# Layer 2 of a two-layer trunk: compression operand layout, branch gates in the key block, second keys among the memory tiles, output projection prepared in steps

## The chip, the cores and the metric

The kernel runs on one core of one Trainium2 chip. The metric is device time in microseconds (us). The kernel before takes 1500.77 us, the median of three runs (1500.14 to 1501.25). The engines are named as in the profile: PE is TensorE's matmul, PEld its weight load, DVE is VectorE, ACT is ScalarE, POOL is GpSimd, and SP issues nearly all DMAs.

## The reference

The input is x of 1024 rows by 1024 columns in float32, and a memory of 256 rows. Both layers norm their input, project it with one wide matrix, run three token mixers, multiply each by its own SiLU gate, and project the concatenation of 1280 columns back to 1024, with a residual. Layer 1 has sliding-window attention, a linear recurrence (RG-LRU) and cross-attention into the memory. The change is in layer 2, whose mixers are HGRN2 (a chunked gated recurrence), native sparse attention (NSA) with 8 query heads in two key groups, and memory cross-attention. What NSA needs of the rest:

```
for t, pe, w1, w2 in keys, values:          # compression: 63 windows of 32 rows, stride 16
    flat = (t windows + pe).reshape(63, 32*64)
    c = silu(flat @ w1) @ w2
g = sigmoid(gate_logits)                    # 24 columns of the input projection
o = g0 * o_compressed + g1 * o_selected + g2 * o_window
```

## The kernel before

Each projection is done three times over: weights and activations are split into a high part and a rest (`split`, L240 on ACT, L246 on DVE or POOL), and `mm3` (L388 to L390) multiplies high by high, high by rest and rest by high. A `block` of weights is loaded in chunks of 512 words per partition: `chunk` issues one DMA for each run of columns (L352) and splits what has landed. With a width of n columns a chunk holds 512/n of the eight contraction slices. `proj_n` multiplies one tile of 128 rows (eight tiles in all) with a block of 256 columns; its result occupies one of three `pj` buffers until it is read out. `proj_t` gives 128 columns transposed for half of the rows (512).

The program writes the work down as generators that `weave` interleaves: a main generator, and sides of which a share falls due as main advances by one yield. A scheduler then fixes the order in which the instructions stand on each engine; each engine runs its own list in order. SP is one list too: a DMA that waits there holds those behind it.

Layer 2 begins while the last matmuls of layer 1's output projection run. `start` makes the first NSA keys and values (`nsa_kv(w, 0)`) and gates. Per tile `nsa_kv` projects, norms (L409, L411), rotates (L421 to L430), scales (L1177), copies the values out (L234, L236), transposes (`pairs`, L249) and stacks the keys (L449, L441). `nsa_gates` computes the 24 branch gates beside it: a separate block of 24 columns, two transposed projections with 24 stationary columns and 512 moving ones, a tanh over 24 by 512, and eight small transposes back. `compress` runs woven into this. For keys and for values it projects, copies the result out as `tT` with the 512 positions of each half-pair in order, moves it by DMA into `U`, and then runs 16 matmuls (L1258) whose moving operand takes every eighth word of `U`, 63 of each group. (In float32 the trace shows two records for each of these 32 matmuls.)

Then `main` runs: NSA with the first keys (65 yields), 4 yields of gates, 20 of memory attention (`pipe(tilesM)`), 9 of the second keys (`nsa_kv(w, 1)`), 4 of gates, 65 of NSA with the second keys. Beside it runs HGRN2 (`self.side`, with quarters due at yields 46, 68, 100 and 138), and the first half of the output projection (`out_proj`), 16 units due between yields 138 and 164. Its first step loads and splits all ten slices of the mixed rows (L1466, L1469, into `mhi` and `mlo`) and the first of four weight blocks. The second half of the output projection stands at the end by itself.

Of the kernel before, what the change touches and what calls it, by code (L numbers as in the profile page):

```python
# [5 lines left out]
F32 = mybir.dt.float32  # L6
# [8 lines left out]
P = 128  # L15
S = 1024
NT = S // P
# [8 lines left out]
LV1 = 4  # L26
T1 = 46
T2 = 68
T3 = 100
T4 = 138  # L30
SIDE = (0, T1, T2, T3, T4)
B_WHO = 6
NR1 = 3
OS = 26
B_PT = 6
B_GT = 1
B_HW = 6
# [11 lines left out]
E0 = 38  # L49
E1 = 46  # L50
E2 = 54
OG = 138
CY = 2
CK = 2
KV2 = 2
# [59 lines left out]
def drain(g):  # L115
    for _ in g:
        pass
# [25 lines left out]
class Trunk:  # L143
# [198 lines left out]
    def chunk(self, k, n, srcs, tag="whl"):  # L342

        nc = self.nc
        view = lambda t: t.rearrange("p (k n) -> p k n", k=k)
        self.nraw += 1
        if self.starting and self.nraw % 3:
            raw = view(self.hw("raw", [H]))
        else:
            raw = view(self.ring.tile([P, H], F32, tag="raw", name=self.uid("raw"), bufs=B_RAW))  # L350
# [3 lines left out]
        t = self.ring.tile([P, 2, H], F32R, tag=tag, name=self.uid("whl"), bufs=B_WHO if tag == 'who' else B_WHL)  # L354
        hi, lo = view(t[:, 0, :]), view(t[:, 1, :])
        self.split(hi[:, :, :n1], lo[:, :, :n1], raw[:, :, :n1])
        return hi, lo

    def block(self, w, pieces, rows=D, n=256, tag="whl"):

        k = H // n
        out = []
        for c in range(rows // (k * P)):
            at, srcs = 0, []
            for col, width in pieces:
                srcs.append((at, width, w[c * k * P:(c + 1) * k * P, col:col + width].rearrange("(k p) n -> p k n", p=P)))
                at += width
            out.append(self.chunk(k, n, srcs, tag))
        return out, k
# [538 lines left out]
    def layer1(self):  # L908
        nc, I, o = self.nc, self.I, OD
        w = I["od_w_in"][0]  # L910
        mix = {i: [None, None] for i in (2, 3, 4)}
        xs = {}

        def norms(half):
            for s in range(4 * half, 4 * half + 4, 2):
                for t in range(s, min(s + 4, 4 * half + 4)):
                    if t not in xs:
                        xs[t] = self.b4([D], name="h")
                        nc.sync.dma_start(xs[t], self.h1[t * P:(t + 1) * P, :])
# [12 lines left out]

        def start():
            yield from self.nsa_kv(w, 0)
            yield from self.gates(w, o["gd"], mix[2])

        first, later, gates = start(), norms(1), self.nsa_gates(w)
        for g in (later, first, first, gates, later, first, first, later, later, gates):
# [12 lines left out]
        drain(self.side)  # L951
        drain(self.out_proj(1, I["od_w_out"][0], 1, self.h1, self.out))

# [188 lines left out]
        nc.sync.dma_start(self.dkn[:, 1, :], I["d_kn_win"][0].partition_broadcast(P))  # L1142
        self.dkv = {}

    def nsa_gates(self, w):
        nc = self.nc
        self.bg = self.lc.tile([P, NT, 24], F32, name="bg")
        blk = self.block(w, [(OD["gate"], 24)], n=64)
        for half in range(2):
            ps = self.pj()  # L1150
            for k in range(KD):
                self.mm3(ps[0:24], self.wk(blk, k, 24), self.xhl(k, half, slice(0, H)), k == 0, k == KD - 1)
            th = self.gt("th", [H])
            nc.scalar.activation(th[0:24], ps[0:24], AF.Tanh, scale=0.5)
            pt = self.tr()
            for i in range(4):
                self.transpose(pt[:, i, 0:24], th[0:24, i * P:(i + 1) * P], 24)
            nc.vector.tensor_scalar(out=self.bg[:, 4 * half:4 * half + 4, :], in0=pt[:, :, 0:24], scalar1=0.5, scalar2=0.5,
                                    op0=ALU.mult, op1=ALU.add)
            yield  # L1160

    def nsa_kv(self, w, g):
        nc, o = self.nc, OD
        kS = [self.b4([S], F32R, name="kS") for _ in range(2)]
        vD = self.b4([NT, 2, HD], name="vD")
        self.dkv[g] = (kS, vD)
        blk = self.n_block(w, *[(o[n] + g * HD, HD) for n in ("ksd", "kwd", "vsd", "vwd")])
        zs, ks = {}, {}
        for s in range(NT + 2):
            if s < NT:  # L1170
                zs[s] = self.proj_n(blk, s)
            if 0 <= s - 1 < NT:
                z = zs.pop(s - 1)
                r = self.heads_norm(z[:, :P], 2, 1.0 / HD, EPS)
                k = self.rope(z[:, :P], 2, self.dkn, s - 1)
                k3 = k[:, :P].rearrange("p (h d) -> p h d", h=2)
                nc.vector.tensor_tensor(out=k3, in0=k3, in1=r[:, :, None].to_broadcast([P, 2, HD]), op=ALU.mult)  # L1177
                self.evac(vD[:, s - 1].rearrange("p b d -> p (b d)"), z[:, P:])
# [29 lines left out]
    def compress(self, w):  # L1208
# [9 lines left out]
        for kind in range(2):  # L1218
            blk = self.t_block(w, o["kcd" if kind == 0 else "vcd"])

            tT = self.tmp.tile([P, 2, H], F32, tag="qk", name=self.uid("tT"), bufs=1)
# [3 lines left out]
            U = self.tmp.tile([P, 2, H], F32, tag="qT", name=self.uid("U"), bufs=2)  # L1225
            for g in range(2):
                for u in range(2):
                    nc.sync.dma_start(U[u * HD:(u + 1) * HD, g, :], tT[g * HD:(g + 1) * HD, u, :])
            nm = "kv"[kind]
            w1 = [self.pt_tile("w1", [4 * 256]).rearrange("p (c n) -> p c n", c=8) for _ in range(2)]  # L1230
            for i in range(2):
                nc.gpsimd.tensor_copy(w1[i][0:1, 0, 0:1], tT[0:1, 0, 0:1])
# [217 lines left out]
        return dict(project=project, turn=turn, choose=choose, coarse=coarse, units=units)  # L1450


    def out_proj(self, l, w, half, resid, dst):

        nc = self.nc
        view = lambda x, q, i: x[half * H + i * P:half * H + (i + 2) * P, q * 256:(q + 1) * 256].rearrange("(i p) n -> p i n", p=P)
        hl, parts = [], (0, 1, 2, 4, 3) if l else range(5)
        for i in range(5):
            hi, lo = (self.b4([2, H], F32R, name=x) for x in ("mhi", "mlo"))
            for c in range(2):  # L1460
# [8 lines left out]
                nc.scalar.copy(hi[:, c, :], m)  # L1469
                nc.vector.tensor_tensor(out=lo[:, c, :], in0=m, in1=hi[:, c, :].bitcast(F32), op=ALU.subtract)  # L1470
            hl.append((hi, lo))
        for q in range(4):
            with self.tc.issue_after(self.loads) if l == 1 and half == 0 else nullcontext():
                blk = self.block(w, [(q * 256, 256)], rows=1280, tag='who' if l == 1 and half == 0 else 'whl')
# [86 lines left out]
```

## Time and profile before

| | us |
|---|---|
| median of three runs | 1500.77 |
| the profiled execution, its own time | 1501.38 |
| span of that execution in the trace | 1499.5 |
| PE busy in the span | 1424.4 (95%) |
| PEld, DVE, POOL, ACT busy | 1233.1, 870.0, 701.1, 657.1 |

Of the chain of work that ended last, the profile gives 82% of the span to PE, 7% to DVE, 4% to ACT and 3% to POOL. Read the table with care: a record of a matmul lasts from its start to its end while the next is already running, so what a matmul costs is the distance from one start to the next, which the timeline gives. The share of busy time is an average; the rows below are from the stages that the change touches.

### The profile page before, as it was taken

The page shows a single profiled execution, that of the slowest core. Times are in us where ns is not written, and L with a number is a line of the kernel's source. Part 1 is how long each engine was busy: PE and PEld are TensorE (multiplying, and loading weights), DVE is VectorE, ACT ScalarE, POOL GpSimd, SP SyncE. Part 2 cuts the span into 40 slices and gives each one's busy share as a digit, 9 for nine tenths or more (in the row PEclk, how much of TensorE's full clock was granted, in tenths as well). Part 3 has the DMA queues.
Part 4 walks back from the last instruction along what each step waited for, and adds up shares of the span by engine and source line. Part 5 has one row for each costly group of instructions (what it writes and reads, how often), then busy time and mean ns, then how long its engine had stood idle before and what let it go on. Part 6 is the DMA issues. An engine that isn't in the chain of part 4 may idle for free.

```text
span 1499.5 us, 27634 instructions
## 1 busy us (share of the span) xinstructions
PE 1424.4 (95%) x10107; PEld 1233.1 (82%) x10107; DVE 870.0 (58%) x2495; ACT 657.1 (44%) x1627; POOL 701.1 (47%) x1124
## 2 busy tenths in 40 slices
PE   7999999998699999999999999999989988899998
PEld 6888878787589988898777877798888866789898
DVE  6667886866763436326565565535664467655621
ACT  7545653645453433114444444423422245655630
POOL 6345675565653243114644444425742456444521
PEclk9999999999799999999999999999999989999999
DMA  8420131022445563310000100031020000423323
GB/s 291 123 65 1 57 85 43 30 64 71 136 132 179 184 168 85 86 41 18 12 22 22 50 8 22 16 91 45 22 78 1 8 1 8 141 66 127 105 82 109
DMA packets 120250, 108.55 MB, mean 72 GB/s; under 512 B 18825, under 2 KB 108466, under 8 KB 120114
## 3 DMA queue, kind: packets, MB, share of 16 engines
q1 hardware_dynamic: 119538, 104.68, 23.4%
q0 software_dynamic: 576, 2.10, 0.5%
q8 instruction: 80, 1.31, 0.4%
q14 instruction: 56, 0.46, 0.1%
HBM read 87.35 MB, written 18.35 MB: 70 GB/s over the span
## 4 chain that ended last, share of the span: by engine, by line
PE 82%; DVE 7%; ACT 4%; POOL 3%; issue 2%; DMA 1%; SPq 0%; ACTq 0%; POOLq 0%; DVEq 0%
PE pj L388 18%; PE pj L389 18%; PE pj L390 17%; PE tr L249 8%; PE ov L1432 5%; PE sc L468 3%; PE sc L469 2%; PE sc L1057 2%; DVE Pt L472 1%; PE sc L1258 1%; PE ov L658 1%; POOL Pt L797 1%; PE ov L805 1%; PE sc L390 1%; PE sc L388 1%
## 5 line engine op out<-in xcount | busy, mean ns | idle before, releaser
L388 PE MATMUL pj<-xn,whl 128*128 128x512 f32 (+1 forms) x536 | 213.4, 399 | 3.6 <-DVE fixed L421 1.4
L389 PE MATMUL pj<-xn,whl 128*128 128x512 f32 (+1 forms) x536 | 213.0, 398 | 0.0
L390 PE MATMUL pj<-xn,whl 128*128 128x512 f32 (+1 forms) x536 | 212.7, 397 | 0.0
L246 POOL TENSOR_TENSOR whl<-raw,whl 128x512 fp32r<-128x512 f32 x98 | 129.9, 1327 | 163.4 <-ACT whl L240 157.3
L388 PE MATMUL pj<-whl,xn 128*128 128x256 f32 x680 | 196.3, 289 | 0.0
L390 PE MATMUL pj<-whl,xn 128*128 128x256 f32 x680 | 196.0, 289 | 0.0
L389 PE MATMUL pj<-whl,xn 128*128 128x256 f32 x680 | 195.9, 288 | 0.0
L388 PE MATMUL pj<-whl,mhi 128*128 128x256 f32 x640 | 185.0, 292 | 11.1 <-ACT mhi L1469 5.3
L240 ACT CAST whl<-raw 128x512 fp32r<-128x512 f32 (+1 forms) x209 | 126.3, 619 | 148.0 <-PE pj L390 62.9
L389 PE MATMUL pj<-whl,mhi 128*128 128x256 f32 x640 | 184.9, 290 | 0.6 <-POOL whl L246 0.6
L390 PE MATMUL pj<-whl,mlo 128*128 128x256 f32 x640 | 182.1, 289 | 0.1
L1412 POOL TENSOR_SCALAR Pt<-Pt,fixed,lc 128x640 f32<-128x640 f32 (+7 forms) x128 | 105.2, 830 | 82.2 <-DVE fixed L1409 67.0
L388 PEld LDWEIGHTS pj<-whl,mhi 128*128 128x128 f32 x640 | 124.7, 196 | 13.4 <-ACT mhi L1469 5.8
L249 PE MATMUL tr<-fixed,Pt 128*128 128x128 f32 x776 | 127.4, 282 | 8.0 <-DVE fixed L472 2.7
L388 PEld LDWEIGHTS pj<-whl,xn 128*128 128x128 f32 x680 | 130.2, 192 | 4.6 <-issue 2.9
L389 PEld LDWEIGHTS pj<-whl,xn 128*128 128x128 f32 x680 | 130.2, 191 | 3.7 <-issue 2.1
L390 PEld LDWEIGHTS pj<-whl,xn 128*128 128x128 f32 x680 | 130.1, 191 | 1.4 <-issue 1.3
L389 PEld LDWEIGHTS pj<-whl,mhi 128*128 128x128 f32 x640 | 125.0, 195 | 3.0 <-issue 2.1
L1408 ACT ACTIVATE Pt<-Pt,fixed 128x640 f32<-128x640 f32 (+7 forms) x128 | 99.0, 775 | 60.4 <-DVE fixed L1405 34.5
L390 PEld LDWEIGHTS pj<-whl,mlo 128*128 128x128 f32 x640 | 123.8, 195 | 1.2 <-issue 0.9
L246 DVE TENSOR_TENSOR whl<-raw,whl 128x512 fp32r<-128x512 f32 x111 | 89.9, 814 | 58.5 <-ACT whl L240 58.2
L388 PEld LDWEIGHTS pj<-xn,whl 128*128 128x128 f32 (+1 forms) x536 | 100.0, 186 | 25.4 <-ACT fixed L409 3.2
(311 smaller groups left out, 3288.7 us busy)
## 6 DMA issues: line engine op xcount, KB each, us to landing
raw<-od_w_in SPq DMA_DIRECT2D x60, 256.0 KB, 3.5
raw<-ev_w_in SPq DMA_DIRECT2D x44, 256.0 KB, 4.3
raw<-ev_w_out SPq DMA_DIRECT2D x40, 256.0 KB, 3.9
raw<-od_w_out SPq DMA_DIRECT2D x40, 256.0 KB, 4.4
mixin<-mix SPq DMA_DIRECT2D x32, 256.0 KB, 3.7
raw<-mem_w_kv SPq DMA_DIRECT2D x16, 256.0 KB, 7.4
x<-x SPq DMA_DIRECT2D x8, 512.0 KB, 6.7
mix<-mix SPq DMA_DIRECT2D x8, 512.0 KB, 3.1
```

The lines of the kernel that those rows point to most:

```text
L240: nc.scalar.copy(hi, src)
L246: eng.tensor_tensor(out=lo, in0=src, in1=hi.bitcast(F32), op=ALU.subtract)
L249: self.nc.tensor.transpose(out=out, in_=in_, identity=self.ident[0:np_, 0:np_])
L388: mm(ps, a[0], b[0], start=first, stop=False)
L389: mm(ps, a[0], b[1], start=False, stop=False)
L390: mm(ps, a[1], b[0], start=False, stop=last)
L468: mm(ps, qT[:, 0, h, :], kS, start=True, stop=False)
L469: mm(ps, qT[:, 1, h, :], kS, start=False, stop=last)
L1057: nc.tensor.matmul(sc[:, i], kx[:, t], qk[:, :, t].rearrange("p a (b w) -> p a b w", w=4 * bm)[:, :, :, bm:], start=True, stop=True)
L1408: nc.scalar.activation(u["Pt"][e][:, :n], u["Pt"][e][:, :n], AF.Exp, bias=nm[:, e:e + 1], accum_out=den[:, e:e + 1], **scale)
L1412: nc.gpsimd.tensor_scalar(out=Pt[:, :n], in0=Pt[:, :n], scalar1=rd[:, e:e + 1], scalar2=gate(2 * hp + e, 1 + b), op0=ALU.mult, op1=ALU.mult)
L1432: nc.tensor.matmul(st["ov"][f * HD:(f + 1) * HD, hp * P:(hp + 1) * P], vD[:, kt, b, :], PT[:, 2 * i + f, :], start=False, stop=b == 0 and ...
```

## The change

The helper `weave` gets a generator form, `woven`, which yields at each yield of its main generator. The rest, in four parts:

1. Compression: `tT` and `U` are stored with the eight residues of the position apart, so the moving operand of each of the 16 matmuls is 63 neighbouring words for each group. The read from PSUM is then strided by 16 words and writes runs of 32.
2. Branch gates: `nsa_gates` goes. Its 24 columns are added to the first key block, which becomes 280 columns wide. A chunk of that block holds one slice, so there are eight chunks with five DMAs each (four of 128 by 64 words, one of 128 by 24), and a buffer tag of their own. The tanh is done per tile on 128 by 24.
3. Second keys: the 9 steps of `nsa_kv(w, 1)` are woven into the memory tiles, between the 14th and the 18th of their 20 yields. `main` is 9 yields shorter, and the later marks are moved.
4. Output projection: loading and splitting the mixed rows becomes `mix_parts`, five steps and a sixth for the first weight block, due between yields 124 and 130; the 16 units are due between 131 and 155.

```diff
-T3 = 100
-T4 = 138
+T3 = 94
+T4 = 129
+KM = (14, 18)
+OP = (124, 130)
-OS = 26
+OS = 24
-OG = 138
+OG = 131
...
 def weave(main, *sides):
+    drain(woven(main, *sides))
+
+
+def woven(main, *sides):
...
                 t[2] += 1
                 next(g, None)
+        yield
...
-            yield from pipe(tilesM)
-            yield from self.nsa_kv(w, 1)
+            yield from woven(pipe(tilesM), (self.nsa_kv(w, 1), 9, *KM))
...
-        weave(main(), (self.side, 90 - SIDE0, *SIDE), (self.out_proj(1, I["od_w_out"][0], 0, self.h1, self.out), 16, OG, OG + OS))
+        hl, wo = [], I["od_w_out"][0]
+
+        weave(main(), (self.side, 90 - SIDE0, *SIDE), (self.mix_parts(1, wo, 0, hl), 6, *OP),
+              (self.out_proj(1, wo, 0, self.h1, self.out, hl), 16, OG, OG + OS))
...
+        pieces = [(o[n] + g * HD, HD) for n in ("ksd", "kwd", "vsd", "vwd")]
+        if g == 0:
+
+            blk = self.block(w, pieces + [(o["gate"], 24)], n=280, tag="whg")
+            self.bg = self.lc.tile([P, NT, 24], F32, name="bg")
+        else:
+            blk = self.n_block(w, *pieces)
...
-                zs[s] = self.proj_n(blk, s)
+                zs[s] = self.proj_n(blk, s, 256 if g else 280)
+                if g == 0:
+                    nc.scalar.activation(self.bg[:, s, :], zs[s][:, 256:], AF.Tanh, scale=0.5)
...
-                self.evac(tT[:, :, half * 256:(half + 1) * 256], self.proj_t(blk, half).rearrange("p (n u) -> p u n", u=2))
+                self.evac(tT[:, :, :, half * 32:(half + 1) * 32], self.proj_t(blk, half).rearrange("p (n j u) -> p u j n", j=8, u=2))
...
-                nc.tensor.matmul(ps, w1[c // 8][:, c % 8, :], U[:, :, c:c + 8 * (NC - 1) + 1:8], start=c == 0, stop=c == 15)
+                nc.tensor.matmul(ps, w1[c // 8][:, c % 8, :], U[:, :, c % 8, c // 8:c // 8 + NC], start=c == 0, stop=c == 15)
```

What the order becomes at three places follows. Lines are those of each kernel (the change shifts them by 4 to 17), numbers behind a name tell buffers apart.

First place, the start of layer 2, on SP: `raw` is a chunk of the first key block, `h_73` the result rows of layer 1 written out, `h_6015` and `h_6022` two row tiles of layer 2 read back in. Before:

```order
L352 DMA raw_6046<-od_w_in 128x2x64 x4
L1487 DMA h_73<-fixed 128x2x256
L352 DMA raw_6054<-od_w_in 128x2x64 x4
L352 DMA raw_6062<-od_w_in 128x2x64 x4
L1479 DMA fixed<-x 128x2x256
L352 DMA raw_6070<-od_w_in 128x2x64
L1487 DMA h_73<-fixed 128x2x256
L352 DMA raw_6070<-od_w_in 128x2x64 x3
L919 DMA h_6015<-h_73 128x1024
L919 DMA h_6022<-h_73 128x1024
L352 DMA raw_6138<-od_w_in 128x8x24
```

The change, from its fourth chunk on:

```order
L359 DMA raw_6073<-od_w_in 128x64 x4
L927 DMA h_6015<-h_73 128x1024
L927 DMA h_6022<-h_73 128x1024
L359 DMA raw_6073<-od_w_in 128x24
L359 DMA raw_6082<-od_w_in 128x64 x4
L359 DMA raw_6082<-od_w_in 128x24
L1504 DMA h_73<-fixed 128x2x256
L927 DMA h_6029<-h_73 128x1024
L927 DMA h_6036<-h_73 128x1024
L359 DMA raw_6091<-od_w_in 128x64 x4
L359 DMA raw_6091<-od_w_in 128x24
L359 DMA raw_6100<-od_w_in 128x64 x4
```

The key block was complete before the first reload of `h`; now the last three of its eight chunks (`raw_6091`, `raw_6100` and `raw_6109`, the last not shown) stand behind all four reloads. On PE the first key tiles then stand so in the change (`pj_6118`, `pj_6144` and `pj_6224` are three row tiles, `whl_6070` and `whl_6079` the third and fourth chunk, `tr` transposes of `h`):

```order
L398 MATMUL pj_6224<-whl_6070,xn_5428 128x280
L396 MATMUL pj_6118<-whl_6079,xn_5427 128x280
L396 MATMUL pj_6144<-whl_6079,xn_5427 128x280
L396 MATMUL pj_6224<-whl_6079,xn_5427 128x280
L256 MATMUL tr_6188<-fixed,h_6015 128x128
L256 MATMUL tr_6197<-fixed,h_6015 128x128
L256 MATMUL tr_6206<-fixed,h_6015 128x128
L256 MATMUL tr_6215<-fixed,h_6015 128x128
L397 MATMUL pj_6118<-whl_6079,xn_5427 128x280
```

Before, each tile ran through all its chunks before the next began; now three tiles advance together, chunk by chunk.

Second place, the end of the second keys on PE: `pj_12006` is the last key tile, each single `tr ... x1` on `fixed` a key transpose, `vm` the memory's values, `pj_12094` the next gate projection. Before:

```order
L249 MATMUL tr_11804<-fixed 128x128
L1057 MATMUL sc_11810<-qk_11590,kx_11645 128x192 x2
L390 MATMUL pj_12006<-whl_11698,xn_6183 128x256
L249 MATMUL tr_11857<-fixed 128x128
L658 MATMUL ov_11606<-PT_11597,vm_10530 64x128 x4
L658 MATMUL ov_11606<-PT_11604,vm_10530 64x128 x4
L249 MATMUL tr_11898<-fixed 128x128
L388 MATMUL pj_12094<-xn_5425,whl_12085 128x512
```

In the change (`pj_12047` is the first of those gate projections):

```order
L396 MATMUL pj_12047<-xn_5431,whl_12043 128x512
L256 MATMUL tr_11890<-fixed 128x128
L397 MATMUL pj_12047<-xn_5432,whl_12043 128x512
L256 MATMUL tr_11896<-fixed,Pt_11403 128x128 x4
L256 MATMUL tr_11903<-fixed,Pt_11403 128x128 x4
L256 MATMUL tr_11955<-fixed 128x128
L398 MATMUL pj_12047<-xn_5431,whl_12043 128x512
```

The key transposes now stand inside a gate projection that does not depend on them, and two memory tiles are still to come.

Third place, the first output-projection matmuls on PE (`mhi` is a slice of mixed rows, L1106, L1100 and L1102 end an HGRN2 unit, L1041 and L1067 are earlier steps of one). Before:

```order
L1106 MATMUL tr_13628<-v_10257,kt_13608 128x128
L1432 MATMUL ov_13335<-PT_13602,vD_11668 64x128 x4
L1102 MATMUL sc_13615<-fixed,qk_13110 128x128
L1100 MATMUL sc_13615<-v_10257,at_13191 128x128
L1102 MATMUL sc_13615<-fixed,qk_13110 128x128
L388 MATMUL pj_13897<-whl_13872,mhi_13816 128x256
```

In the change:

```order
L1436 MATMUL ov_12954<-PT_13121,vD_11460 64x128 x4
L1436 MATMUL ov_12954<-PT_13195,vD_11460 64x128 x2
L396 MATMUL pj_13918<-whl_13802,mhi_13541 128x256
L396 MATMUL pj_13989<-whl_13802,mhi_13541 128x256
L1321 MATMUL sc_13199<-lc_5203,qT_13130 128x63
L1067 MATMUL sc_13226<-qk_13089,kx_13165 128x192 x2
```

The first output matmuls stood behind the last step of HGRN2's last unit but for its final transposes; now they stand among that unit's earlier steps, 12 of them at first, 6 and 6 later, and the long run of them where it was.

## Rows read from the trace of the kernel before

**Rows 1.** The page, part 1: busy us, share of the span, instructions.

```profile
PE 1424.4 (95%) x10107; PEld 1233.1 (82%) x10107; DVE 870.0 (58%) x2495; ACT 657.1 (44%) x1627; POOL 701.1 (47%) x1124
```

**Rows 2.** Windows: length, busy PE, PEld, DVE, ACT, POOL, granted clock, DMA.

```profile
545.00:557.00 12.00, 12.00 (x81) 8.80 (x80) 5.66 (x19) 5.19 (x13) 7.80 (x15) 1.00 0.58 180
600.00:700.00 100.00, 100.00 (x563) 86.47 (x562) 36.49 (x113) 21.87 (x60) 21.50 (x37) 1.00 0.18 48
1110.00:1120.00 10.00, 5.27 (x29) 4.00 (x28) 9.56 (x35) 2.81 (x10) 7.26 (x15) 0.83 0.34 97
1280.00:1290.00 10.00, 6.07 (x41) 5.20 (x40) 7.55 (x19) 6.65 (x14) 7.98 (x19) 0.85 0.79 253
1290.00:1300.00 10.00, 10.00 (x71) 10.00 (x71) 7.09 (x14) 4.79 (x8) 1.64 (x3) 0.80 0.61 193
```

**Rows 3.** Timeline of PE: start, us, line, tile, count, idle time before and releaser.

```profile
1114.71 0.30 PE L249 MATMUL tr<-fixed 128*128 128x128 f32 x1 [3.34 <-DVE fixed L1177]
1116.40 0.76 PE L388 MATMUL pj<-xn,whl 128*128 128x512 f32 x1 [1.39 <-DVE vD L236]
...
1287.83 1.01 PE L388 MATMUL pj<-whl,mhi 128*128 128x256 f32 x3 [3.61 <-ACT whl L240]
```

**Rows 4.** Groups by line and shape on PE: count, busy us, mean ns.

```profile
L388 PE MATMUL pj<-xn,whl 128*24 128x512 f32 x16 | 6.4, 400 | 0.8 <-ACT xn L330 0.8
L249 PE MATMUL tr<-fixed,th 24*128 24x24 f32 x8 | 0.8, 220 | 0.0
```

**Rows 5.** Timeline of PE, one gate projection and one key projection.

```profile
574.53 0.40 PE L389 MATMUL pj<-xn,whl 128*24 128x512 f32 x1
574.77 0.39 PE L390 MATMUL pj<-xn,whl 128*24 128x512 f32 x1
...
585.06 0.28 PE L389 MATMUL pj<-whl,xn 128*128 128x256 f32 x1
585.18 0.28 PE L390 MATMUL pj<-whl,xn 128*128 128x256 f32 x1
```

**Rows 6.** Timeline of PEld, the compression matmuls of the values.

```profile
653.10 6.37 PEld L1258 LDWEIGHTS sc<-U,w 128*128 128x128 f32 x28
659.49 0.21 PEld L388 LDWEIGHTS pj<-whl,xn 128*128 128x128 f32 x1
```

**Rows 7.** Timeline of PE, float32 matmuls with 128 neighbouring moving columns.

```profile
758.28 0.39 PE L1102 MATMUL sc<-fixed,qk 128*128 128x128 f32 x2
758.50 0.39 PE L1100 MATMUL sc<-v,at 128*128 128x128 f32 x2
```

**Rows 8.** Group by line and shape on ACT, window 560 to 680.

```profile
L409 ACT ACTIVATE fixed<-pj 128x128 f32<-128x128 f32 x5 | 1.4, 278 | 6.7 <-PE pj L390 6.7
L234 ACT COPY tT<-pj 128x512 f32<-128x512 f32 x2 | 1.2, 587 | 5.1 <-PE pj L390 5.1
```

**Rows 9.** Timeline of PE, layer 2's first matmul.

```profile
540.83 0.28 PE L388 MATMUL pj<-whl,xn 128*128 128x256 f32 x1
```

**Rows 10.** Timeline of SP at the start of layer 2.

```profile
527.56 4.15 SPq L352 DMA_DIRECT2D raw<-od_w_in  x8
...
541.49 0.37 SPq L1487 DMA_DIRECT2D h<-fixed  x1
544.66 0.81 SPq L919 DMA_DIRECT2D h<-h  x2
545.52 0.98 SPq L352 DMA_DIRECT2D raw<-od_w_in  x2
```

**Rows 11.** DMA issues: count, KB each, median us to landing.

```profile
raw<-od_w_in SPq DMA_DIRECT2D x32, 64.0 KB, 2.4
```

**Rows 12.** One line on ACT, window 480 to 600: ns min, median, max.

```profile
L240 ACT CAST whl<-raw x30: 337/620/637, 483.6 to 597.3; 128x512 fp32r<-128x512 f32 x29, 128x192 fp32r<-128x192 f32 x1
```

**Rows 13.** Timeline of PE, a step of HGRN2's last unit.

```profile
1258.18 0.89 PE L1057 MATMUL sc<-qk,kx 128*128 128x192 f32 x4 [2.52 <-DVE qk L1052]
```

**Rows 14.** Timeline of SP, the first loads of mixed rows in layer 2.

```profile
1280.65 1.27 SPq L1466 DMA_DIRECT2D mixin<-mix  x3
```

More of the change, by code (lines that the diff above doesn't have):

```diff
@@ L347, in chunk @@
         if self.starting and self.nraw % 3:
-            raw = view(self.hw("raw", [H]))
+            raw = view(self.hw("raw", [k * n]))
         else:
-            raw = view(self.ring.tile([P, H], F32, tag="raw", name=self.uid("raw"), bufs=B_RAW))
+            raw = view(self.ring.tile([P, H], F32, tag="raw", name=self.uid("raw"), bufs=B_RAW)[:, :k * n])
         for at, width, ap in srcs:
@@ L353, in chunk @@
         n1 = srcs[-1][0] + srcs[-1][1]
-        t = self.ring.tile([P, 2, H], F32R, tag=tag, name=self.uid("whl"), bufs=B_WHO if tag == 'who' else B_WHL)
+        t = self.ring.tile([P, 2, k * n], F32R, tag=tag, name=self.uid("whl"), bufs=B_WHO if tag == 'who' else B_WHL)
         hi, lo = view(t[:, 0, :]), view(t[:, 1, :])
@@ L935, in start @@
             yield from self.gates(w, o["gd"], mix[2])
-        first, later, gates = start(), norms(1), self.nsa_gates(w)
-        for g in (later, first, first, gates, later, first, first, later, later, gates):
+        first, later = start(), norms(1)
+        for g in (later, first, first, later, first, first, later, later):
             next(g)
@@ L1143, in nsa_setup @@
         self.dkv = {}
[L1145 to L1160, printed above, removed]
     def nsa_kv(self, w, g):
@@ L1170, in nsa_kv @@
             if s < NT:
-                zs[s] = self.proj_n(blk, s)
+                zs[s] = self.proj_n(blk, s, 256 if g else 280)
+                if g == 0:
+                    nc.scalar.activation(self.bg[:, s, :], zs[s][:, 256:], AF.Tanh, scale=0.5)
+                    if s % 4 == 3:
+                        nc.vector.tensor_scalar(out=self.bg[:, s - 3:s + 1, :], in0=self.bg[:, s - 3:s + 1, :], scalar1=0.5, scalar2=0.5,
+                                                op0=ALU.mult, op1=ALU.add)
             if 0 <= s - 1 < NT:
@@ L1177, in nsa_kv @@
                 nc.vector.tensor_tensor(out=k3, in0=k3, in1=r[:, :, None].to_broadcast([P, 2, HD]), op=ALU.mult)
-                self.evac(vD[:, s - 1].rearrange("p b d -> p (b d)"), z[:, P:])
+                self.evac(vD[:, s - 1].rearrange("p b d -> p (b d)"), z[:, P:256])
                 ks[s - 1] = k
@@ L1219, in compress @@
             blk = self.t_block(w, o["kcd" if kind == 0 else "vcd"])
-            tT = self.tmp.tile([P, 2, H], F32, tag="qk", name=self.uid("tT"), bufs=1)
+            tT = self.tmp.tile([P, 2, 8, 64], F32, tag="qk", name=self.uid("tT"), bufs=1)
             for half in range(2):
-                self.evac(tT[:, :, half * 256:(half + 1) * 256], self.proj_t(blk, half).rearrange("p (n u) -> p u n", u=2))
+                self.evac(tT[:, :, :, half * 32:(half + 1) * 32], self.proj_t(blk, half).rearrange("p (n j u) -> p u j n", j=8, u=2))
                 yield
-            U = self.tmp.tile([P, 2, H], F32, tag="qT", name=self.uid("U"), bufs=2)
+            U = self.tmp.tile([P, 2, 8, 64], F32, tag="qT", name=self.uid("U"), bufs=2)
             for g in range(2):
                 for u in range(2):
-                    nc.sync.dma_start(U[u * HD:(u + 1) * HD, g, :], tT[g * HD:(g + 1) * HD, u, :])
+                    nc.sync.dma_start(U[u * HD:(u + 1) * HD, g], tT[g * HD:(g + 1) * HD, u])
             nm = "kv"[kind]
@@ L1231, in compress @@
             for i in range(2):
-                nc.gpsimd.tensor_copy(w1[i][0:1, 0, 0:1], tT[0:1, 0, 0:1])
+                nc.gpsimd.tensor_copy(w1[i][0:1, 0, 0:1], tT[0:1, 0, 0, 0:1])
                 nc.sync.dma_start(w1[i], I[f"d_w1{nm}"][0, i * 1024:(i + 1) * 1024, :].rearrange("(c p) n -> p c n", p=P))
@@ L1450, in nsa_tile, with mix_parts @@
         return dict(project=project, turn=turn, choose=choose, coarse=coarse, units=units)
-    def out_proj(self, l, w, half, resid, dst):
+    def mix_parts(self, l, w, half, hl):
         nc = self.nc
-        view = lambda x, q, i: x[half * H + i * P:half * H + (i + 2) * P, q * 256:(q + 1) * 256].rearrange("(i p) n -> p i n", p=P)
-        hl, parts = [], (0, 1, 2, 4, 3) if l else range(5)
         for i in range(5):
@@ L1471, in out_proj, with w_out @@
             hl.append((hi, lo))
+            yield
+        hl.append(self.w_out(l, w, half, 0))
+        yield
+    def w_out(self, l, w, half, q):
+        with self.tc.issue_after(self.loads) if l == 1 and half == 0 else nullcontext():
+            return self.block(w, [(q * 256, 256)], rows=1280, tag='who' if l == 1 and half == 0 else 'whl')
+    def out_proj(self, l, w, half, resid, dst, hl=None):
+        nc = self.nc
+        view = lambda x, q, i: x[half * H + i * P:half * H + (i + 2) * P, q * 256:(q + 1) * 256].rearrange("(i p) n -> p i n", p=P)
+        parts = (0, 1, 2, 4, 3) if l else range(5)
+        if hl is None:
+            hl = []
+            drain(self.mix_parts(l, w, half, hl))
         for q in range(4):
-            with self.tc.issue_after(self.loads) if l == 1 and half == 0 else nullcontext():
-                blk = self.block(w, [(q * 256, 256)], rows=1280, tag='who' if l == 1 and half == 0 else 'whl')
+            blk = hl.pop() if q == 0 else self.w_out(l, w, half, q)
             for i in range(4):
```

1 line of the change is left out of this document (removed).

## The prediction, made before the changed kernel was run

> **What bounds the kernel now.** I read the page's busy shares first: PE is busy for 1424.4 of the span's 1499.5 us [rows 1], and 82% of the chain that ended last is PE. So a matmul that goes is worth what it holds the PE for, unless a wait takes its place. Then the windows by stage: while compression runs the PE is busy for 100 of 100 us at full clock [rows 2], and so it is where layer 2 begins. Where the second keys end and where the last projection begins it is busy for 5.27 and 6.07 of 10 us [rows 2]. Then the timeline of PE, for the distance from one start to the next, which is what a matmul costs (a record of 400 ns hides a distance of 235), and for the idle time before an instruction: 3.34 and 1.39 us at the end of the second keys, 3.61 us before the first output matmul [rows 3]. [...] Last SP's timeline where layer 2 begins, because the change puts more DMAs into that list.
>
> **The sum's base.** Durations come from one execution, whose own time is 1501.38 us; its span is 1499.5, and the 1.9 us around it stay. It lies 0.6 us above the median of 1500.77, so I take 0.6 off at the end.
>
> **Gates.** Three lines with 16 matmuls each go, 48 with 24 stationary and 512 moving columns [rows 4]. Two starts lie 0.24 us apart [rows 5], rounded; I take 0.235, and 48 of them are 11.3 us, on the path, since nothing else holds the PE there. The eight small transposes were 0.8 us [rows 4]. Added are 24 columns on 192 matmuls. The distance is 0.12 us for 256 moving columns and 0.235 for 512 [rows 5], so 24 columns are 0.115 by 24/256, or 0.011 us, and 192 of them 2.1 us. Net gain 10.0 us. The eight narrow tanhs replace two wide ones on ACT, which is busy for 22 of 100 us there [rows 2]; I put them at nothing, and price below the moment in which they are not hidden.
>
> **The first key block arrives late.** This is the wait the change adds. Before, 16 DMAs brought the block, and one the gate columns. Now 40 do, and the last 15 stand on SP behind the reloads of `h`, which are issued at 544.66 and take 0.81 us [rows 10]; those wait for the result rows of 541.49 [rows 10] and cannot be earlier. Eight pieces of 64 KB took 4.15 us to issue, 0.52 each [rows 10]. For pieces of 32 KB and 12 KB no row exists; the shortest issues in those rows are 0.37, and I take 0.5, near the row of the same kind. So the last piece is issued at 545.5 + 7.5 = 553.0, lands after 2.4 us [rows 11], and is split in some 0.7 us (a cast of 192 words 0.34 [rows 12], the subtraction as long): 556.1. Then the last nine of the 72 matmuls of the three tiles follow, 1.2 us: 557.3. PE starts with these tiles at 540.83 [rows 9] and has in that time 72 by 0.131, 9.4 us, and 16 transposes of 128 columns, at 0.11 [rows 7] 1.8 us. It idles for 16.5 - 11.2 = 5.3 us, where it now is busy throughout [rows 2].
> What stands behind it: all three `pj` buffers fill at the same moment, and the fourth tile waits until ACT has read out the first. ACT's list has six reads first (three tanhs, three squares), at 0.28 [rows 8] 1.7 us. The clock adds 1.7 us, which is what 4.7 us of waiting cost at the second keys (0.17 of 10 us [rows 2]). Together 8.7 us of the 10.0. Ends: 0.37 a piece and no loss of clock, 4; 0.6 a piece and twice the loss, 12.
> [...] No run shows pieces of 32 KB yet.
>
> **Compression.** The 64 records are 0.228 us apart: 28 loads take from 653.10 to 659.49 [rows 6]. Float32 matmuls with the same stationary size and 128 neighbouring moving columns are 0.11 apart, four in 0.44 (758.28 to 758.50 is two) [rows 7]. If the step of eight words is what doubles it, 64 by 0.118 is 7.6 us, all on the path, since the PE is full [rows 2]. If the weights are, it is 0. I take 7.6: the rows differ in the step and hardly in anything else. `tT` is written by four copies, of 587 ns on ACT [rows 8]; even doubled they cost 2.4 us off the PE, while the PE has other matmuls before the first use (its window has no idle time).
> [...]
>
> **Second keys.** Their last transposes wait 3.34 us for DVE, and the gate projection behind them 1.39 us for a `pj` buffer [rows 3]; with the clock's 1.7 us that is 6.4 us. In the new order those transposes stand inside a projection that does not need them, and memory tiles are left to fill in. The work on DVE and ACT is the same but falls on memory tiles, where they are needed too. What is late next is the memory's own softmax. Ends 0 and 6.4; I take 4.5.
>
> **Output projection.** Before it begins PE waits 3.61 us for the first weights' cast [rows 3], which queues on ACT with ten casts of mixed rows; the clock is 0.85 and 0.80 in the two windows, 3.5 us more [rows 2]. Together 7.1. The first slices are now due five yields of `main` earlier than before (125 against 139, less the 9 that left `main`), the weights when they were; in steps they no longer queue all at once. But 12 early output matmuls now stand in the PE's list before HGRN2's last steps; if their rows are not there, the steps wait too. Ends -3.6 (a wait as long, elsewhere) and 7.1; I take 5.
>
> Sum: 10.0 - 8.7 + 7.6 + 4.5 + 5 = 18.4 us; 1501.38 - 18.4 - 0.6 = 1482.4, and I say 1482. Its own range is 1474 to 1491. Anything within 0.2%, 3 us, of 1500.77 could not be told from no change.
>
> **Rivals.**
> Moved waits: the waits at keys and output projection come back between the same engines. DVE is busy for 9.56 of 10 us at the end of the keys [rows 2], which speaks for it; the new filler between speaks against it. Then 10.0 - 8.7 + 7.6 = 8.9, 1491.9. Chance 0.19.
> The compression operand does nothing: the distance stays 0.228. Against it is [rows 7]. 1490. Chance 0.05.
> The start is covered: pieces issue in 0.37 us, the three tiles are waited for by 4 us, and the keys and output waits go in full: 10.0 - 4 + 7.6 + 6.4 + 7.1 = 27, 1474. Chance 0.10.
> Slower: the early output matmuls block the PE. They now stand among the steps of HGRN2's last unit, one of which ran at 1258.18 [rows 13], while the first mixed rows were asked for at 1280.65 [rows 14] and the first output matmul was ready at 1287.83 [rows 3]. If the loads came as late as that, PE would wait some 30 us where other work stands behind it, and 5 us of the gain would go as well: 1482.4 + 5 + 22 (eight of the 30 are waits there already) makes 1509. It decides from a wait of about 14 us on. Against it: the first loads are due five yields earlier. Chance 0.09.
>
> **How the numbers follow.** The forecast has 0.57. The range is 1469 to 1498: it takes in the covered start, the moved waits and the dead operand, and leaves out the slower case and the far ends. Faster by over 0.2%: the four cases that lie below 1497.8 have 0.91, less 0.05 for their bad ends: 0.86. Same: 0.05. Slower: 0.09.
>
> **What would show it.** Compression: records of 0.11 us distance on the matmul that reads `U`. Gates: no matmul with 24 stationary columns, and 280-column ones 0.131 apart. Start: PE idle between 541 and 559 with the wait put down to a split or a DMA of the key block, 5 to 7 us in all, and SP issuing pieces until about 553. Keys: no wait for the last key transposes. Output: its first matmuls among HGRN2 steps with a wait under 3 us. I am wrong if the start is waited for by more than 15 us, if the distance stays, or if a wait of over 10 us stands before the first `mhi` matmul.

## The result, and the profile of the changed kernel

The changed kernel takes 1484.5 us (median of 4 runs, 1481.0 to 1487.4) against 1501.0 for the kernel before (4 runs, 1500.1 to 1504.1): ratio 0.9885, 95% interval 0.9863 to 0.9907, 16.5 us faster. The forecast was 1482. A later set of 6 runs gave 1485.7 and 0.9904 (0.9887 to 0.9922). The profiled execution is the one of 1481.0 us.

Page, part 1, of the changed kernel (answers to [rows 1]):

```profile
PE 1406.0 (95%) x10051; PEld 1222.1 (83%) x10051; DVE 865.2 (58%) x2497; ACT 657.6 (44%) x1636; POOL 709.6 (48%) x1125
```

PE is busy for 18.4 us less and no other engine for more than 9 us more. Windows of the changed kernel, columns as in [rows 2]:

```profile
400.00:410.00 10.00, 10.00 (x94) 9.07 (x95) 9.16 (x19) 6.03 (x12) 7.87 (x17) 1.00 0.81 262
545.00:557.00 12.00, 8.10 (x34) 6.70 (x33) 4.22 (x13) 5.95 (x20) 6.89 (x12) 0.66 0.47 115
1110.00:1120.00 10.00, 10.00 (x62) 7.93 (x59) 4.07 (x7) 1.44 (x5) 0.62 (x1) 1.00 0.35 105
1200.00:1300.00 100.00, 84.96 (x630) 69.63 (x628) 64.22 (x209) 49.04 (x120) 54.07 (x92) 0.90 0.21 68
```

and two of the kernel before that [rows 2] do not hold:

```profile
400.00:410.00 10.00, 9.59 (x62) 8.40 (x63) 7.38 (x14) 5.42 (x11) 6.83 (x14) 0.68 0.85 267
1200.00:1300.00 100.00, 83.18 (x628) 68.67 (x627) 71.22 (x256) 51.30 (x143) 57.56 (x112) 0.91 0.15 48
```

Three things are to be seen. The start of layer 2, full before, now has idle time and a granted clock of 0.66. The second keys' hole (5.27 of 10 us before) is gone; the same window holds later work in the change, so the key transposes themselves follow below. The stage of the last projection has hardly changed: 84.96 of 100 us against 83.18. The first row of each is in layer 1, which the change doesn't touch: there the clock was lower in the profile of before (0.68 against 1.00), and layer 1 ended at 540.7 us against 537.3. The same changed kernel profiled once more ended it at 541.0, and over all profiles of this document it ended between 537.1 and 543.1, with the same list of matmuls. Such differences are scatter, so I compare stages by their lengths, counted from the last matmul of layer 1's projection, not by clock time:

| kernel | to the last `U` matmul | from there to the last matmul | sum |
|---|---|---|---|
| before | 118.8 | 835.8 | 954.6 |
| changed | 108.8 | 829.3 | 938.1 |
| changed, profiled again | 109.0 | 829.7 | 938.8 |

(Differences of starts on PE: 540.7, 659.5 and 1495.3 in the kernel before; 537.3, 646.1 and 1475.4 in the changed one.) The change takes 10.0 us up to the end of compression and 6.5 behind it. Windows over the second of these stages, first before, then changed:

```profile
659.49:1495.30 835.81, 797.12 (x5965) 684.11 (x5964) 455.50 (x1529) 350.94 (x902) 387.88 (x646) 0.98 0.16 47
646.11:1475.43 829.32, 796.64 (x5967) 683.27 (x5965) 454.18 (x1529) 350.76 (x902) 395.39 (x646) 0.98 0.16 48
```

PE idles there for 38.7 us before and 32.7 in the change, which is nearly all of the 6.5. The clock took no part: its stretches at the lower level (a granted clock of 0.50, as from 741 to 747 us in the kernel before) add up to 34.1 us in either profile.

The last two key transposes of the second keys in the change stand inside a gate projection and wait for nothing:

```profile
1097.11 0.27 PE L256 MATMUL tr<-fixed 128*128 128x128 f32 x1
1097.13 0.48 PE L397 MATMUL pj<-xn,whl 128*128 128x512 f32 x1
...
1098.32 0.27 PE L256 MATMUL tr<-fixed 128*128 128x128 f32 x1
```

Between 1080 and 1110 us PE idles twice, for 1.50 and 0.56 us, both times for a result of DVE: less than half of the two waits before (3.34 and 1.39).

The start in the changed kernel, timeline of PE, columns as in [rows 3]:

```profile
537.44 0.29 PE L396 MATMUL pj<-whl,xn 128*128 128x280 f32 x1
...
539.37 0.29 PE L396 MATMUL pj<-whl,xn 128*128 128x280 f32 x1
...
547.18 0.65 PE L396 MATMUL pj<-whl,xn 128*128 128x280 f32 x3 [2.04 <-ACT whl L247]
549.95 0.60 PE L397 MATMUL pj<-whl,xn 128*128 128x280 f32 x1 [0.30 <-POOL whl L253]
...
550.58 0.43 PE L397 MATMUL pj<-whl,xn 128*128 128x280 f32 x1
550.81 0.43 PE L398 MATMUL pj<-whl,xn 128*128 128x280 f32 x1
...
552.65 1.06 PE L396 MATMUL pj<-whl,xn 128*128 128x280 f32 x3 [0.94 <-ACT whl L247]
555.72 0.60 PE L396 MATMUL pj<-whl,xn 128*128 128x280 f32 x1 [0.61 <-ACT vD L241]
```

and of SP (answers to [rows 10]):

```profile
519.45 4.67 SPq L359 DMA_DIRECT2D raw<-od_w_in  x10
...
538.10 0.38 SPq L1504 DMA_DIRECT2D h<-fixed  x1
540.33 0.80 SPq L927 DMA_DIRECT2D h<-h  x2
541.18 5.67 SPq L359 DMA_DIRECT2D raw<-od_w_in  x10
...
547.27 2.72 SPq L359 DMA_DIRECT2D raw<-od_w_in  x6
550.44 1.75 SPq L359 DMA_DIRECT2D raw<-od_w_in  x3
```

Fifteen matmuls take 1.93 us, 0.129 each; where the clock is at its lower level (0.50 from 549 to 557 us) they stand 0.23 apart (550.58 to 550.81). The waits are the forecast ones, three put down to the key block's splits and one to `vD` for a `pj` slot: 3.9 us in all. SP issues ten pieces in 4.67 us, 0.47 apart. The ten behind the reloads take 5.67 because two of them wait, 1.1 us together. The key block's last piece is the fifth of the six behind 547.27, issued at 549.1; the pieces after it belong to the next block.

Compression, timeline of PEld (answers to [rows 6]):

```profile
642.88 3.32 PEld L1262 LDWEIGHTS sc<-U,w 128*128 128x128 f32 x28
646.12 0.19 PEld L396 LDWEIGHTS pj<-whl,xn 128*128 128x128 f32 x1
```

28 loads in 3.24 us are 0.116 apart, where it was 0.228. The copies that write `tT` in the new order, groups by shape on DVE and ACT (answer to [rows 8]), cost what they did:

```profile
L243 DVE COPY tT<-pj 128x512 f32<-128x512 f32 x2 | 1.4, 692 | 3.2 <-PE pj L398 3.2
L241 ACT COPY tT<-pj 128x512 f32<-128x512 f32 x2 | 1.2, 592 | 4.8 <-PE pj L398 4.8
```

The last projection's stage, timeline of PE (answers to [rows 3, 13]):

```profile
1223.29 0.44 PE L1436 MATMUL ov<-PT,vD 128*64 128x128 f32 x4 [2.32 <-ACT PT L1428]
1223.89 0.51 PE L396 MATMUL pj<-whl,mhi 128*128 128x256 f32 x2 [0.16 <-ACT whl L247]
1226.15 1.65 PE L1067 MATMUL sc<-qk,kx 128*128 128x192 f32 x4 [1.59 <-DVE qk L1062]
...
1270.71 0.63 PE L256 MATMUL tr<-fixed,at 128*128 128x128 f32 x4 [1.99 <-DVE at L1128]
1271.95 0.39 PE L396 MATMUL pj<-whl,mhi 128*128 128x256 f32 x1 [0.61 <-ACT mhi L1472]
```

The wait of 3.61 us for the first weights is gone and the first output matmul starts at 1223.9 among HGRN2's steps, but waits for `PT`, `qk` and `at` stand around it. Behind the last key transpose PE idles for 18.1 us in all, where behind the same point before (1116.4) it idled for 18.8.

### The profile page after: what moved, and what is told of

Its sections match the earlier page's. It is cut to its first block, busy times and chain, and to the rows that moved or that the text cites. A ratio compares the mean times of both kernels' runs of the same rounds, so it can differ in the third digit from the quotient of the medians.

```text
span 1479.2 us, 27613 instructions
## 1 busy us (share of the span) xinstructions
PE 1406.0 (95%) x10051; PEld 1222.1 (83%) x10051; DVE 865.2 (58%) x2497; ACT 657.6 (44%) x1636; POOL 709.6 (48%) x1125
## 4 chain that ended last, share of the span: by engine, by line
PE 80%; DVE 8%; POOL 4%; ACT 3%; issue 3%; DMA 2%; SPq 1%; ACTq 0%; DVEq 0%; POOLq 0%
PE pj L396 17%; PE pj L397 17%; PE pj L398 17%; PE tr L256 8%; PE ov L1436 5%; PE sc L476 3%; PE sc L477 3%; DVE Pt L480 2%; PE sc L1067 1%; PE ov L813 1%; PE ov L666 1%; PE sc L398 1%; DMA mixin<-mix 1%; PE sc L396 1%; PE sc L397 1%
## 5 line engine op out<-in xcount | busy, mean ns | idle before, releaser
L398 PE MATMUL pj<-xn,whl 128*128 128x512 f32 x520 | 206.5, 397 | 0.0
L396 PE MATMUL pj<-xn,whl 128*128 128x512 f32 x520 | 206.3, 397 | 0.0
L397 PE MATMUL pj<-xn,whl 128*128 128x512 f32 x520 | 206.0, 396 | 0.0
L396 PE MATMUL pj<-whl,xn 128*128 128x256 f32 (+1 forms) x680 | 197.0, 293 | 3.6 <-ACT whl L247 3.0
L397 PE MATMUL pj<-whl,xn 128*128 128x256 f32 (+1 forms) x680 | 197.4, 291 | 0.3 <-POOL whl L253 0.3
L398 PE MATMUL pj<-whl,xn 128*128 128x256 f32 (+1 forms) x680 | 196.3, 290 | 0.0
L253 POOL TENSOR_TENSOR whl<-raw,whl 128x512 fp32r<-128x512 f32 (+1 forms) x99 | 130.6, 1320 | 124.7 <-ACT whl L247 118.0
L253 DVE TENSOR_TENSOR whl<-raw,whl 128x512 fp32r<-128x512 f32 (+1 forms) x113 | 93.7, 832 | 68.0 <-ACT whl L247 67.7
L1428 ACT COPY PT<-tr 128x512 f32<-128x512 f32 (+1 forms) x152 | 75.5, 530 | 114.1 <-PE tr L256 113.2
```

Source lines behind the costliest of these rows:

```text
L253: eng.tensor_tensor(out=lo, in0=src, in1=hi.bitcast(F32), op=ALU.subtract)
L396: mm(ps, a[0], b[0], start=first, stop=False)
L397: mm(ps, a[0], b[1], start=False, stop=False)
L398: mm(ps, a[1], b[0], start=False, stop=last)
L1428: nc.scalar.copy(PT[:, :2 * len(grp)], pt[:, :2 * len(grp)])
```

## The experiments

Each was timed beside the kernel before on its chip. Stage lengths are from one profile of each, as in the table above.

| kernel | median us | before beside it | ratio (95%) | to last `U` | behind it | sum |
|---|---|---|---|---|---|---|
| compression only | 1492.5 | 1501.1 | 0.9944 (0.9927-0.9962) | 111.4 | 834.3 | 945.7 |
| gates only | 1487.2 | 1501.1 | 0.9905 (0.9885-0.9926) | 116.6 | 824.9 | 941.5 |
| gates, joined DMAs | 1486.8 | 1501.1 | 0.9906 (0.9888-0.9924) | 109.1 | 830.6 | 939.7 |
| keys only | 1496.5 | 1501.1 | 0.9976 (0.9960-0.9992) | 118.6 | 831.3 | 949.8 |
| output only | 1510.8 | 1500.4 | 1.0080 (1.0059-1.0101) | 119.1 | 844.6 | 963.7 |
| compression + gates | 1479.1 | 1500.4 | 0.9864 (0.9846-0.9882) | 108.7 | 827.0 | 935.7 |
| change, output undone | 1483.2 | 1500.4 | 0.9884 (0.9867-0.9900) | 108.9 | 829.7 | 938.7 |
| change, keys undone | 1481.8 | 1500.4 | 0.9877 (0.9854-0.9899) | 109.4 | 829.4 | 938.9 |
| turn only | 1492.0 | 1500.2 | 0.9950 (0.9935-0.9965) | 119.2 | 825.2 | 944.4 |
| compr. + gates, turn undone | 1496.9 | 1500.2 | 0.9980 (0.9967-0.9993) | 110.4 | 839.5 | 949.9 |
| compr. + gates, joined DMAs | 1479.9 | 1500.2 | 0.9871 (0.9853-0.9888) | 101.4 | 826.8 | 928.2 |
| whole change again | 1485.7 | 1500.2 | 0.9904 (0.9887-0.9922) | 109.0 | 829.7 | 938.8 |

**Compression only.**

```diff
-for c in range(16): matmul(ps, w1[...], U[:, :, c:c + 8 * (NC - 1) + 1:8], ...)
+for c in range(16): matmul(ps, w1[...], U[:, :, c % 8, c // 8:c // 8 + NC], ...)
```

> The kernel before, with nothing changed but the layout of tT and U in the compression, so that the 64 moving operands of 2 by 63 columns lie side by side instead of eight words apart. TensorE's list of instructions is word for word the old one. Step theory: the 64 records come 0.11 us apart instead of 0.228, 64 by 0.118 is 7.6 us, and the time is 7.6 us (0.5%) under the kernel before. Weights theory: the distance stays 0.228 and the time is the same within 1 us. Cover theory: the distance halves, but a wait for the strided evictions of tT (longer on ACT and DVE) or for the first weights of the next stage takes 3 us or more of it back.

The distance halves, to 0.116 us (28 loads in 3.24). 8.5 us by the medians, 7.3 of them up to the last `U` matmul: the step theory, shown alone, since PE's list is otherwise unchanged. Behind compression nothing is given back (834.3 against 835.8), so the cover theory falls.

**Gates only, and with joined DMAs.** The gates' part of the diff alone; and the same with the block loaded so:

```diff
+rg = ring.tile([P, KD, 24]); dma_start(rg, w[:, gate columns])            # one DMA
+for c in range(4):
+    raw = view(ring.tile([P, H]), 2); four dma_start of [P, 2, 64]        # 16 DMAs
+    split(hi[:, :, :256], lo[:, :, :256], raw)
+    split(hi[:, :, 256:], lo[:, :, 256:], rg[:, 2 * c:2 * c + 2])
```

> The kernel before, with the branch gates in the first key block (280 columns, 40 DMAs instead of 17) and nothing else. Forecast's terms: 10.0 us of TensorE work go, 8.7 come back as a wait at the start of layer 2 (5.3 idle between 541 and 559, 1.7 for a pj slot, 1.7 of clock), so 1.3 us under the kernel before. Covered start: the wait is 4 us or less in all and the time 6 us under. Larger stall: the wait costs 12 us and the time is 2 us above.

> As the gates alone, but the block is loaded in 17 DMAs: four chunks of two row blocks, each in four pieces of 64 KB as before, and the 24 gate columns in one piece of their own; the chunks still have 280 columns and the matmuls are the same. Queue theory: the start waits because SP issues 40 pieces half a microsecond apart; with 17 the last is issued about 11 us earlier, the idle time between 541 and 559 goes (under 1 us), the clock stays up, and the time is 7 to 9 us below that of the gates alone and 8 to 10 below the kernel before. Late data theory: TensorE waits there because the block's splits queue on ACT and POOL or because of the reloads of h; the same 4 to 6 us of idle time stay and the time is that of the gates alone within 2 us.

Windows of PE at the start, the gates alone:

```profile
545.00:557.00 12.00, 7.32 (x54) 6.52 (x52) 2.51 (x3) 3.52 (x7) 5.18 (x8) 1.00 0.61 154
557.00:570.00 13.00, 12.29 (x58) 11.18 (x59) 9.52 (x28) 7.42 (x24) 10.54 (x16) 0.74 0.61 184
```

With 17 DMAs:

```profile
545.00:557.00 12.00, 12.00 (x91) 11.70 (x91) 9.21 (x26) 8.65 (x25) 10.36 (x18) 1.00 0.67 214
557.00:570.00 13.00, 12.51 (x71) 10.45 (x70) 12.24 (x32) 7.36 (x22) 5.68 (x11) 1.00 0.30 89
```

Up to the last `U` matmul both theories' local numbers hold: the gates alone gain 2.2 us (1.3 forecast), joined 9.7; the queue costs 7.5 (8.7 forecast). But the gates alone are 14 us faster in time, and 10.9 of those lie behind compression, where nothing was changed by hand; the joined ones are level with them, having lost 5.7 us there. Both expectations missed this. The joined ones have no wait at the second keys either, so their loss lies elsewhere; it was not followed.

**Keys only.**

```diff
-yield from pipe(tilesM); yield from self.nsa_kv(w, 1)
+yield from woven(pipe(tilesM), (self.nsa_kv(w, 1), 9, *KM))
```

> The kernel before, with the second group's key and value block woven into the memory tiles (and the marks of the side streams moved by the nine steps that main loses), nothing else. Forecast: the waits of 3.34 and 1.39 us at the end of the second keys go, with 1.7 us of clock; 4.5 us net (0 to 6.4) under the kernel before. Moved waits theory: those two waits go, but as much appears on DVE's results among the memory tiles, and the time is that of the kernel before within 1.5 us.

4.5 us by the medians, 4.7 by the stages, in line with the forecast.

**Output only.** The diff's `mix_parts` on the kernel before, with `OP = (131, 137)`.

> The kernel before with the last projection prepared in steps (mixed rows and first weights at steps 131 to 137 of main, the projection from 138 as before) and nothing else. Forecast: 5 us under the kernel before (ends -3.6 and 7.1), the wait of 3.61 us for the first weights' cast gone. No-worth theory: that wait goes, but its time turns up as waits of TensorE among the HGRN2 steps and the second selection; the kernel before within 1.5 us.

10.5 us slower. The times of both theories fall; the waits that the second foretold are there, and cost more than the wait that went. Timeline of PE there:

```profile
1247.95 1.15 PE L1436 MATMUL ov<-PT,vD 128*64 128x128 f32 x12 [1.77 <-ACT PT L1428]
1260.11 0.44 PE L250 MATMUL tr<-fixed,Pt 128*128 128x128 f32 x2 [2.83 <-POOL Pt L1416]
1269.41 0.35 PE L389 MATMUL pj<-whl,mhi 128*128 128x256 f32 x1 [1.05 <-DVE fixed L1413]
1278.46 0.66 PE L1436 MATMUL ov<-PT,vD 128*64 128x128 f32 x8 [1.68 <-ACT PT L1428]
...
1293.97 0.38 PE L389 MATMUL pj<-whl,mhi 128*128 128x256 f32 x1 [1.40 <-ACT mhi L1472]
1300.80 1.11 PE L250 MATMUL tr<-fixed,at 128*128 128x128 f32 x4 [3.18 <-DVE at L1122]
```

The output matmuls come early and the second selection's and HGRN2's own steps late: HGRN2's last matmul that reads `qk` and `kx` starts 744.2 us after layer 1's end, where it was 731.1. Before that matmul stand 54 output matmuls; in the kernel before it was none, in the change 18. Behind compression PE idles for 43.9 us (38.7 before), and the clock is at its lower level for 41.0 (34.1). That is the prediction's slower rival in kind (early output work in front of other steps), not by its wait of 30 us.

**Compression + gates; the change without its output part; without its keys part.**

> Compression operands and gates together on the kernel before: the change without its keys and its output part. Additive theory (from the two single runs, ratios 0.9944 and 0.9905): 1501 by 0.985 is 1478.5, some 6 us under the changed kernel, so the other two parts cost time there. Forecast's terms: 10.0 - 8.7 + 7.6 is 8.9 us, 1492, and keys and output bring the rest. Between: the gates alone gained 8 us in the second keys only because all that stands behind an edit is sorted anew; then this kernel, sorted another way, need not have that gain, and lies anywhere from 1479 to 1492 with 9 to 10 us of gain up to the end of compression in any case.

> The changed kernel with the last projection as it was: mixed rows and first weights prepared at its first step, at the old distance from the end (mark 129, 26 steps). Forecast: the change's output part is worth 5 us, so 1489.5, with a wait of 3 to 4 us for the first weights' cast before the first mhi matmul. No-worth theory: the waits of that stage come from the serial steps of HGRN2 and of the second selection and not from the preparation; 1484.5 within 2 us.

> The changed kernel with the second key block behind the memory tiles again, in front of the gate projection, and the marks nine steps later (103, 138; mixed rows from 131 to 137, output from 138 over 26 steps). Forecast: keys are worth 4.5 us, so 1489; the waits before the last key transposes come back (3.3 and 1.4 us). Luck theory: what stands behind an edit is sorted anew, and those waits were absent in the gates alone with the keys in their old place; then 1484.5 within 2 us.

The two first parts alone give 1479.1, the additive theory. Taking either of the other two out of the change moves nothing: 829.7 and 829.4 behind compression against 829.3. With both out it is 827.0. So inside the change the keys and the output are worth nothing each. With the keys undone the wait of 1.39 us stays away and that of 3.34 is 0.74, on the side of the luck theory.

**The turn.** What did the gates do 500 us later? `split` gives its subtraction to VectorE and GpSimd in turn, by a counter; before, layer 2's start has five splits ahead of the rest, now eight. An odd shift swaps the turn of every split behind it.

```diff
+self.nlo += 3
 first, later, gates = start(), norms(1), self.nsa_gates(w)
```

> The kernel before with one number changed: the counter by whose turn a split's subtraction goes to VectorE or to GpSimd starts layer 2 three higher, which is where the gates edit leaves it (five splits become eight). No work is added, removed or moved by hand. Turn theory: that alone makes the list of the second keys come out as in the gates alone (last key transposes inside the projections), the waits of 3.34 and 1.39 us go, and the time is 6 to 9 us under the kernel before, all of it won behind 1085 us and nothing before the end of compression. Luck theory: the gain of the gates alone in that stage came from the sorting as a whole or from the freed TensorE time; here within 2 us of the kernel before.

> Compression operands and gates together, with that counter one higher at the start of layer 2, so that the turns fall as in the kernel before. Turn theory: the waits at the second keys come back and the time is 6 to 9 us above the 1479 of the two parts, 1485 to 1488, with the gain of 9 to 10 us up to the end of compression unchanged. Luck theory: 1479 within 2 us.

One counter takes 8.2 us by the medians, all behind compression (825.2 against 835.8; up to there 119.2 against 118.8). Timeline of PE at the second keys, the kernel before with only the turn swapped (answers to the first two of [rows 3]):

```profile
1108.35 0.27 PE L249 MATMUL tr<-fixed 128*128 128x128 f32 x1
1108.38 0.37 PE L390 MATMUL pj<-whl,xn 128*128 128x256 f32 x1
...
1108.82 0.27 PE L249 MATMUL tr<-fixed 128*128 128x128 f32 x1
...
1115.94 0.30 PE L249 MATMUL tr<-fixed 128*128 128x128 f32 x1 [0.17 <-DVE fixed L1178]
```

and DVE's splits of weights near them, there:

```profile
1114.45 0.69 DVE L246 TENSOR_TENSOR whl<-raw,whl 128x512 fp32r<-128x512 f32 x1
1118.97 0.68 DVE L246 TENSOR_TENSOR whl<-raw,whl 128x512 fp32r<-128x512 f32 x1
```

and in the kernel before:

```profile
1104.43 0.68 DVE L246 TENSOR_TENSOR whl<-raw,whl 128x512 fp32r<-128x512 f32 x1
1109.17 0.69 DVE L246 TENSOR_TENSOR whl<-raw,whl 128x512 fp32r<-128x512 f32 x1 [0.52 <-ACT whl L240]
```

The last key transposes now stand among projections, as in the gates alone. The subtractions that DVE gets fall elsewhere: before, in front of the last keys' steps on DVE, now between those steps; that this place makes the order is not shown. The two waits were 4.7 of the 10.6 us behind compression, and PE's idle time there falls by 4.9 (38.7 to 33.8). The rest goes with the clock: 20.5 us at its lower level instead of 34.1, and only 3.4 of that difference lie at the second keys. Undone on top of compression and gates, the turn brings the waits back (3.16 and 1.39 us on the same tiles). That costs 17.9 us by the medians, twice what was expected. The two spans differ by 19.4: 12.5 behind compression, 1.7 between layer 1's end and there, and 5.3 in layer 1, where PE's list is the same in both and the clock was at its lower level for 30.7 us against 10.2. So at most some 14 us of it can be put down to the turn. That the turn decides is shown in both directions; by what weighing the sorting of the lists comes to another order was not followed.

**Joined DMAs on compression + gates, and the whole change again.**

> Compression operands and gates together, with the first key block loaded in 17 DMAs instead of 40 and nothing else moved. Queue theory: the start's idle time and its slow clock go (some 6 us) and stay gone: 1473. Given-back theory (as gates joined against gates alone, 7.5 us ahead at the end of compression and level at the end): the last projection then waits longer for its first weights, and the time is 1479 within 2 us.

> The changed kernel once more, on the chip and beside the runs of the two parts with 17 DMAs. The earlier ratios to the kernel before were 0.9885 for the whole change and 0.9864 for compression and gates alone. If the keys and output parts cost time on top of those two, its ratio stays at 0.988 to 0.990; if the difference was scatter, 0.986 to 0.987.

The profile has the 7.3 us of the start, and keeps them (826.8 behind compression against 827.0); the times do not show them: 0.9871 against 0.9864. In that profile layer 1 ended at 542.8 us, 5.7 later than in the other one. Whether joining the DMAs slows layer 1, or one profile of each misleads, stays open; with 40 DMAs too layer 1 ended as late as 543.1 (keys undone). The waits for the first output weights, which the given-back theory names, are 4.6 us there against 4.1, too little to give 7 us back. The whole change, with 0.9904, lies on the side of a cost of the keys and output parts, and is 5.8 us slower than the two parts with joined DMAs on the same chip; those two intervals just touch.

## Why the prediction came out, step by step

**Compression, 7.6.** Right: 7.3 by the stage, and the distance 0.116. That the step sets the distance was an estimate from [rows 6] and [rows 7]; the operand change alone, with PE's list as it was, shows it for words 32 bytes apart against neighbouring ones, with 0.228 against 0.116. No run tried a step between the two, so where the distance begins to grow is not shown here.

**Gates 10.0 and start -8.7.** Right in both sizes: net 2.2 against 1.3, the queue 7.5 against 8.7, the key block's last piece issued 11.8 us after layer 1's last matmul against 12.3 (553.0 less 540.7). The split between idle time and clock was not right. Idle time is 3.9 us in the change, 0.6 of it for the `pj` slot, where the forecast had 5.3 and 1.7, and the sign "5 to 7 us in all" failed. The clock took more: in the gates alone the windows hold 5.4 us of idle time against 0.5 with joined DMAs, which leaves 2.6 of the 7.5 to the clock (1.7 forecast; its mean over the second window, 13 us, was 0.74 there against 1.00). Pieces of 32 and 12 KB were issued 0.47 us apart where none waited, against 0.52 for 64 KB [rows 10], so half the size saves hardly any of the issue.

**Second keys, 4.5.** Right for that edit alone (4.5). In the change it earned nothing, because the gates edit had already removed the same two waits through the turn (in compression + gates, with the keys in their old place, 0.17 us of them is left). The step that failed is "in the new order those transposes stand inside a projection": they did without it. I read the order of the whole change against before, and put the difference down to the edit that names the keys.

**Output projection, 5.** Wrong. Alone it costs 10.5 us, in the change nothing that can be measured. The step that failed is counting the 3.61 us wait and its clock as gained: the wait did go, but PE waits for the second selection's and HGRN2's steps instead (84.96 of 100 us busy against 83.18, and 18.1 us idle behind the keys against 18.8). That the early output matmuls push those steps back I read from the starts of the output-only run (13.1 us later, with 54 output matmuls in front); no run tested it by itself. The earlier casts and splits on ACT, DVE and POOL are a rival that was not tested either.

**The sum.** The first three terms, 8.9, measured 10.0. The last two, 9.5, measured 6.5, but from another source: the turn, which the prediction does not have, gives 10.6 behind compression by itself (8.2 in time), and the parts that were meant to give 9.5 add nothing to that. So the total came out partly by luck: 1482 was near while its last two terms were wrong as causes, and the rival of moved waits, 1491.9, was right on the keys and output themselves and wrong on the time. The first half of the change alone, compression and gates, comes out lower (1479, 2.4 us less by the stages); its interval overlaps that of the whole in the first set of runs.

## What to carry to other kernels

Where a scheduler sorts the lists and a counter deals work to engines in turn, an edit in one place deals out everything behind it anew: read such counters before crediting a far gain to a near edit, and test each edit alone. Before preparing a late stage early, look which serial steps its matmuls would then overtake. A moving operand read eight words apart doubled the distance of the float32 matmuls here (0.228 us against 0.116), and turning the layout in the copy that writes it cost nothing (592 ns against 587 on ACT, 692 in both on DVE).

## What the runs showed of the hardware that I had not expected

Reading PSUM in steps of 16 words instead of 2 cost the copies nothing: 692 ns on DVE, as before, and 592 against 587 on ACT. By the medians of the changed kernel's DMA issues, pieces of 12 KB in rows of 96 bytes seem to land later than larger ones (count, KB each, median us to landing):

```profile
raw<-od_w_in SPq DMA_DIRECT2D x32, 32.0 KB, 2.0
raw<-od_w_in SPq DMA_DIRECT2D x16, 64.0 KB, 2.3
raw<-od_w_in SPq DMA_DIRECT2D x8, 12.0 KB, 3.2
```

Their place in the queue explains it better than their size. The trace has the landing of only three of the eight: 1.8, 3.2 and 3.5 us, and the 32 KB pieces issued just in front of the two late ones took 3.5 and 3.8.
